# The MLP's relu outputs stored from ScalarE's queue, and the MLP's raw weights loaded and released in halves of a quarter

## Chip, core and metric

The kernel runs on one core of a Trainium2 chip. The metric is the device time of one launch in microseconds (us); the time before is the median of three runs. Engines are named as the profile does: PE is TensorE, DVE is VectorE, ACT is ScalarE, POOL is GpSimd, SP is SyncE. SP computes nothing here; it issues DMAs. ACT and POOL compute and can issue DMAs as well.

## What is computed

One transformer block on 512 tokens of width 2048, in float32: a mixing part (attention with compressed, selected and windowed keys, beside a retention part), then an MLP of hidden width 8192. The change touches the MLP alone:

```python
mix = jnp.concatenate([o_a.astype(x.dtype), o_r], axis=-1) @ w_out[l]
x = x + rms_norm(mix, norm_mix_post[l])
h = rms_norm(x, norm_mlp_pre[l])
u = jnp.square(jax.nn.relu(h @ w_up[l]))          # (512, 2048) @ (2048, 8192)
x = x + rms_norm(u @ w_down[l], norm_mlp_post[l])  # (512, 8192) @ (8192, 2048)
```

## The kernel before

**Precision.** Every float32 operand of a matmul is split into a high part (a cast on ACT to the reduced float32 type, tile `whi`) and a low part (the difference, a subtract on DVE, tile `wlo`). A product is three matmuls: high by high, low by high, high by low (`mm3`).

**Seven products for eight.** Both MLP matmuls are done block by block with the scheme of seven products on 2 by 2 blocks. A block of weights has four raw quarters, named 11, 12, 21 and 22, of 1 MB each ([128, 2048] float32). The products are numbered 0 to 6 and done in the order 0, 1, 2, 5, 4, 3, 6 (`ORDER`). Their weight operands are quarter 11, then 21, then 11 with 12 added, then 22, then 11 with 22 added, then 12 with 22 added, then 11 with 21 added (`ADD` names the quarter added to and the one that is added, `SPLIT` the one that is split). The adds run on DVE in place (L951). In most blocks the add of product 3 is instead a DMA from POOL that accumulates quarter 22 from HBM onto quarter 12 (`late_sum`, L917).

**Phases and slabs.** A product is a phase, and a phase is two slabs (s = 0 and 1), each half of the contraction, of [128, 1024] raw weights and 24 matmuls. `Feed` walks the phases. For a slab `advance` emits the add on DVE (if any), the cast on ACT (L956), and then the subtract on DVE of the slab before (`low`, L931). `slab` keeps it three slabs ahead of the matmuls at most; `whi` and `wlo` have three buffers each. The order of the instructions on each engine is the order in which this code emits them; nothing reorders them.

**Slots.** Raw quarters live in four slots of 1 MB: `low0`, `low1` and two rows of the tile `Y` (three more, `pre0` to `pre2`, are used once at the start). A quarter's slot is given back in `low`, after the subtract of slab 1 of the last phase that uses the quarter. `load` then issues the next quarter from SP (L925), in the order of the phases, up to three phases ahead (`ahead`).

**Up and down.** The up part has 16 blocks of 512 hidden columns, in the order 0, 4, 1, 5, 2, 6, 3, 7, 8, ..., 15. Products 0 and 1 of blocks 0 to 3 and product 0 of block 4 are done early, while the normalisation of the mixing part is still being finished on ACT and DVE (`work3`); their slabs have their own loads. So blocks 0 to 3, when their turn comes, have five phases left: 5, 2, 4, 3, 6. From product 5, which needs 22, such a block goes on to product 2, which needs both 11 and 12. The down part has 16 pieces of seven phases.

**Stores.** Each up block leaves seven hidden tensors, [128, 512] each. One is squared relu of product 1's sum, one of product 4's, one of product 3's (`hidden`: relu and square on ACT, L1122 and L1123, one slab later, the store two slabs after that). Four are sums of them (`sums`, four DVE adds, L1181 to L1184, stored one slab later). `keep_u` (L1126) stores each to `ud` in HBM from SP, 112 stores of 256 KB in all. The down part loads them back (`u_operand`).

**DMA semaphores.** DMAs of the SP and ACT queues share eight completion semaphores (DMAHW0 to DMAHW7), handed round in the order in which the code emits the DMAs. A DMA that takes a semaphore waits until the DMA eight before it, of either queue, has landed, unless its engine already knows that. POOL's DMAs have eight of their own (DMASW).

Of the kernel before, what the change touches and what calls it, by code (L numbers as in the profile page):

```python
# [10 lines left out]
F32 = mybir.dt.float32  # L11
F32R = mybir.dt.float32r
AF = mybir.ActivationFunctionType
ALU = mybir.AluOpType
AX = mybir.AxisListType.X

P = 128
# [95 lines left out]
def block_kernel(ctx: ExitStack, tc: tile.TileContext, x, norm_mix_pre, w_in, cmp_pe_k, cmp_w1_k, cmp_b1_k,  # L113
                 cmp_w2_k, cmp_pe_v, cmp_w1_v, cmp_b1_v, cmp_w2_v, t5_bias, w_out, norm_mix_post, norm_mlp_pre,
                 w_up, w_down, norm_mlp_post, c_rot, c_dec, c_hot, c_misc, out):
    nc = tc.nc
# [22 lines left out]
    ud = dram.tile([7, DFF // 512, P, 512], F32, name="ud")  # L139
# [242 lines left out]
    for q in (2, 3):  # L382
        c = slice(q * 512, (q + 1) * 512)
# [19 lines left out]
    for n in range(4 * NT):  # L403
        t, q = n // 4, n % 4
# [398 lines left out]
    Y = fp.tile([P, NT, DM], F32, name="Y")  # L803
# [60 lines left out]
    ADD = (None, None, (11, 12), (12, 22), (11, 22), None, (11, 21))  # L864
    SPLIT = (11, 21, 11, 12, 11, 22, 11)
    SL = 1024
# [11 lines left out]
    class Ring:  # L878
# [3 lines left out]
        def take(self):  # L882
            self.views.append(self.views.pop(0))
            return self.views[-1]

    class Feed:


# [1 line left out]


        def __init__(self, phases, slots, ahead, short):
            self.phases, self.free, self.ahead, self.lent = phases, list(slots), ahead, []
            self.short = short
            self.n, self.at, self.R, self.ready = 0, 0, {}, {}
            self.loads, self.last = [], {}
            for i, (g, prod, source) in enumerate(phases):
                for q in (SPLIT[prod],) if self.by_dma(i) else (ADD[prod] or ()) + (SPLIT[prod],):
                    if (g, q) not in self.last:
                        self.loads.append((g, q, source, i))  # L900
                    self.last[g, q] = i
            self.held = None

# [5 lines left out]
        def late_sum(self, i):  # L909

            g, prod, source = self.phases[i]
            to, by = ADD[prod]
            src = source(by)
            k = src.shape[1]
            r = self.R[g, to].rearrange("p (k n) -> p k n", k=k)
            for h in (slice(0, k // 2), slice(k // 2, k)):
                nc.gpsimd.dma_start(r[:, h], src[:, h], accum_op=ALU.add)  # L917

        def load(self, most=99):
            while most and self.loads and self.free and self.loads[0][3] <= self.n // 2 + self.ahead:  # L920
                most -= 1
                g, q, source, _ = self.loads.pop(0)
                r = self.R[g, q] = self.free.pop(0)
                src = source(q)
                nc.sync.dma_start(r.rearrange("p (k n) -> p k n", k=src.shape[1]), src)  # L925

        def low(self):
            if self.held is None:
                return
            hi, lo, src, i, s = self.held  # L930
            nc.vector.tensor_sub(lo, src, hi.bitcast(F32))  # L931
            self.ready[2 * i + s] = (hi, lo)
            self.held = None
            if s:
                for q in (11, 12, 21, 22):
                    if self.last.get((self.phases[i][0], q)) == i:
                        r = self.R.pop((self.phases[i][0], q))
                        if all(r is not o for o in self.lent):
                            self.free.append(r)

        def advance(self):
            self.load()
            if self.n == 2 * len(self.phases):
                self.low()
                return
            i, s = divmod(self.n, 2)
            g, prod, _ = self.phases[i]
            c = slice(s * SL, (s + 1) * SL)
            if ADD[prod] and not self.by_dma(i):
                to, by = (self.R[g, q][:, c] for q in ADD[prod])  # L950
                nc.vector.tensor_add(to, to, by)  # L951
            src = self.R[g, SPLIT[prod]][:, c]
            o = 40 if isinstance(g, int) and prod == 6 and s else 0
            hi = hp.tile([P, SL + 128], F32R, name="whi")[:, o:o + SL]
            lo = hp.tile([P, SL + 128], F32R, name="wlo")[:, o:o + SL]
            nc.scalar.copy(hi, src)  # L956
            self.low()
            self.held = hi, lo, src, i, s
            self.n += 1
            if prod == 2 and s and (j := [j for j in range(i, min(i + 5, len(self.phases))) if self.by_dma(j)]):  # L960
                self.late_sum(j[0])
# [137 lines left out]
    NPRO = 4  # L1099
# [3 lines left out]
    phases = [((b, p), p, up_source(b)) for b, p in early]  # L1103
# [19 lines left out]
        nc.scalar.activation(v, v, AF.Square)  # L1123

    def keep_u(k, b, v):
        nc.sync.dma_start(ud[k, b], v)  # L1126

    def up_done(b, p, ps):

# [86 lines left out]
        feed.low()  # L1216
        yield

    feed.load(1)
    for q in range(4):  # L1220
        x_fetch(0, q)
    feed.load(1)
    outs = [x1_out(t) for t in range(NT)]
    beside(ends[0][1](), 2, primed())
    beside(ends[1][1](), 1, x1_chain(0))
# [8 lines left out]
    sxv = [sxp.tile([P, 8, 2 * P], F32R, name=f"sx{i}") for i in range(2)]  # L1234
    prctx = ExitStack()
    prp = prctx.enter_context(tc.tile_pool(name="prim", bufs=1, reuse_waits="tile"))
    feed.lent = [prp.tile([P, 2048], F32, name=f"pre{i}") for i in range(3)]
    feed.free = feed.lent + feed.free
    XA = [tuple(H[:, 0:8, 0:256] for H in (Hh, Hl)), tuple(H[:, 8:16, 0:256] for H in (Hh, Hl)),
          tuple(H[:, 0:8, 256:512] for H in (Hh, Hl)), (sxv[0], sxv[1]), None, None,  # L1240
# [20 lines left out]
    def work3():  # L1261
        yield from pieces("addadaadaa", a=outs[2], d=x1_chain(3))
        yield from both(x1_sums(0), outs[3])
        feed.free += [Y[:, 0, :], Y[:, 2, :]]
        yield from x1_sums(1)

    feed.ahead = len(early)
# [220 lines left out]
```

## Time and profile before

| | us |
|---|---|
| median of 3 runs | 2223.9 (2223.78 to 2226.18) |
| the profiled execution | 2220.96 |
| its span, first to last instruction | 2219.2 |
| PE busy | 2161.8 (97%) |
| DVE busy | 1575.4 (71%) |
| ACT busy | 994.2 (45%) |
| granted TensorE clock, mean | 0.994 |

The span is the time on the core between the first and the last instruction that the profiler recorded; 1.76 us of the execution lie around it. Idle time of PE is 57.4 us in the whole span. The mixing part ends at about 937 us, the up part runs to about 1574 us, the down part's matmuls to about 2200 us, and what follows is the end of the output on DVE. A row of an idle engine names what ended the wait last; a row of DVE or ACT that waits for a DMA names the tile that the DMA fills.

### The profile page before, as it was taken

To read this page: it belongs to the slowest core of one execution; us is meant where nothing else is said; L and a number is where in the kernel's file an instruction comes from. 1 tells how busy PE (TensorE), PEld (TensorE's weight loads), DVE (VectorE), ACT (ScalarE), POOL (GpSimd) and SP (SyncE) were. 2 spreads that over 40 slices of the span, in tenths; PEclk is the share of its full clock that TensorE was granted. 3 is DMA by queue.
4 is the path that set the end of the run, shared out by engine and by line. 5 is a ranking of instruction groups with operands and counts; after the bars stand their busy time and mean duration, and the time that the engine had idled before them with its cause. 6 is when DMAs were issued, how large, how long until landed. Compare 5 with 4: busy or idle time off the path is not lost.

```text
span 2219.2 us, 31801 instructions
## 1 busy us (share of the span) xinstructions
PE 2161.8 (97%) x12787; PEld 1915.4 (86%) x12787; DVE 1575.4 (71%) x1880; ACT 994.2 (45%) x1440; POOL 111.1 (5%) x131
## 2 busy tenths in 40 slices
PE   8999999999999999989999999999999999999995
PEld 7888878878778899989999999999888888888874
DVE  6213555554556533598888878878879999999998
ACT  5213343343332323575555555555664454445443
POOL 0000000000000000000000000000000000000001
PEclk9999999999999999999999999999999999999998
DMA  6543324323224334565655766767675656566664
GB/s 192 136 122 88 93 65 95 95 72 91 81 72 138 98 103 142 186 221 171 207 172 169 225 179 183 190 174 209 223 229 161 216 163 218 160 197 175 192 187 86
DMA packets 248054, 342.67 MB, mean 154 GB/s; under 512 B 14011, under 2 KB 159755, under 8 KB 247009
## 3 DMA queue, kind: packets, MB, share of 16 engines
q1 hardware_dynamic: 213440, 292.43, 40.6%
q0 software_dynamic: 24368, 36.67, 10.3%
q10 hardware_dynamic: 10098, 11.55, 1.5%
q8 instruction: 100, 1.64, 0.3%
q14 instruction: 48, 0.39, 0.1%
HBM read 298.85 MB, written 41.75 MB: 153 GB/s over the span
## 4 chain that ended last, share of the span: by engine, by line
PE 87%; DVE 8%; ACT 2%; issue 1%; DMA 1%; POOL 0%; SPq 0%; DVEq 0%; POOLq 0%; ACTq 0%
PE prod L156 16%; PE prod L155 16%; PE prod L154 16%; PE mm L154 11%; PE mm L156 11%; PE mm L155 11%; DVE wlo L931 2%; PE S L583 2%; PE S L706 1%; PE PT L646 1%; PE oT L741 1%; PE oT L501 1%; PE oT L154 1%; DVE Y L951 1%; DMA low<-in_w_up 1%
## 5 line engine op out<-in xcount | busy, mean ns | idle before, releaser
L956 ACT CAST whi<-low 128x1024 fp32r<-128x1024 f32 x230 | 242.1, 1053 | 277.5 <-PE prod L156 134.9
L155 PE MATMUL prod<-wlo,Hh 128*128 128x512 f32 x896 | 350.5, 391 | 11.5 <-DVE wlo L931 11.4
L956 ACT CAST whi<-Y 128x1024 fp32r<-128x1024 f32 x212 | 222.6, 1050 | 285.7 <-PE prod L156 119.9
L144 DVE TENSOR_TENSOR wlo<-raw,whi 128x1024 fp32r<-128x1024 f32 (+4 forms) x152 | 168.6, 1113 | 255.4 <-ACT whi L143 250.6
L156 PE MATMUL prod<-whi,Hl 128*128 128x512 f32 x896 | 349.4, 390 | 0.0
L154 PE MATMUL prod<-whi,Hh 128*128 128x512 f32 x896 | 349.3, 390 | 0.0
L931 DVE TENSOR_TENSOR wlo<-low,whi 128x1024 fp32r<-128x1024 f32 x230 | 280.1, 1221 | 48.2 <-ACT whi L956 47.3
L156 PE MATMUL prod<-Hh,wlo 128*128 128x256 f32 x1024 | 285.3, 279 | 13.4 <-DVE wlo L931 13.4
L931 DVE TENSOR_TENSOR wlo<-Y,whi 128x1024 fp32r<-128x1024 f32 x212 | 258.4, 1221 | 38.7 <-ACT whi L956 37.7
L154 PE MATMUL prod<-Hh,whi 128*128 128x256 f32 x1024 | 284.7, 278 | 0.3 <-ACT Hh L143 0.3
L155 PE MATMUL prod<-Hl,whi 128*128 128x256 f32 x1024 | 284.0, 277 | 0.9 <-DVE Hl L144 0.9
L143 ACT CAST whi<-raw 128x1024 fp32r<-128x1024 f32 (+4 forms) x152 | 145.6, 960 | 302.2 <-PE mm L155 148.0
L154 PE MATMUL mm<-whi,Hh 128*128 128x416 f32 (+4 forms) x704 | 263.1, 374 | 0.5 <-ACT Hh L143 0.5
L156 PE MATMUL mm<-whi,Hl 128*128 128x416 f32 (+4 forms) x704 | 248.6, 353 | 0.5 <-DVE Hl L144 0.5
L155 PE MATMUL mm<-wlo,Hh 128*128 128x416 f32 (+4 forms) x704 | 248.1, 352 | 0.0
L156 PE MATMUL prod<-sx,wlo 128*128 128x256 f32 x768 | 212.3, 276 | 2.6 <-DVE wlo L931 2.6
L154 PE MATMUL mm<-Hh,whi 128*128 128x512 f32 x512 | 214.7, 419 | 0.1
L154 PE MATMUL prod<-sx,whi 128*128 128x256 f32 x768 | 212.0, 276 | 0.0
L155 PE MATMUL prod<-sx,whi 128*128 128x256 f32 x768 | 212.0, 276 | 0.0
L155 PEld LDWEIGHTS prod<-wlo,Hh 128*128 128x128 f32 x896 | 168.7, 188 | 49.7 <-DVE wlo L931 14.8
L156 PEld LDWEIGHTS prod<-Hh,wlo 128*128 128x128 f32 x1024 | 192.9, 188 | 15.3 <-DVE wlo L931 15.2
L156 PE MATMUL mm<-Hh,wlo 128*128 128x512 f32 x512 | 200.5, 392 | 0.0
(265 smaller groups left out, 3969.9 us busy)
## 6 DMA issues: line engine op xcount, KB each, us to landing
raw<-in_w_in SPq DMA_DIRECT2D x160, 256.0 KB, 3.1
low<-in_w_up SPq DMA_DIRECT2D x38, 1024.0 KB, 6.0
Y<-in_w_up SPq DMA_DIRECT2D x32, 1024.0 KB, 6.3
Y<-in_w_down SPq DMA_DIRECT2D x32, 1024.0 KB, 5.2
low<-in_w_down SPq DMA_DIRECT2D x32, 1024.0 KB, 5.2
Y<-ud SPq DMA_DIRECT2D x49, 512.0 KB, 9.0
ud<-Y SPq DMA_DIRECT2D x77, 256.0 KB, 4.3
raw<-in_w_out SPq DMA_DIRECT2D x32, 416.0 KB, 3.5
```

What stands on the lines that cost most here:

```text
L143: nc.scalar.copy(hi, src)
L144: nc.vector.tensor_sub(lo, src, hi.bitcast(F32))
L154: nc.tensor.matmul(ps, ah, bh, start=first, stop=False)
L155: nc.tensor.matmul(ps, ah, bl, start=False, stop=False)
L156: nc.tensor.matmul(ps, al, bh, start=False, stop=last)
L501: nc.tensor.matmul(hid[:65, :DK], kv[:, l:l + STRIDE * 64 + 1:STRIDE], w1s[l // 16][:, l % 16, :], start=l == 0, stop=l == CBLK - 1)
L583: nc.tensor.matmul(sps[:, :c + L], QT[g][:, h, qs], k, start=True, stop=True)
L646: nc.tensor.transpose(pt[:, e * P:(e + 1) * P], Pt[:, e, rows_of(j)], ident)
L706: nc.tensor.matmul(sps[:, :n], QK[:, 2 + d, rows_of(j)], QK[:, d, j * P:], start=d == 0, stop=d == 1)
L741: nc.tensor.matmul(o[:, :DR], AT[:, a0:a0 + P], vr[:, j, :], start=j == 0, stop=j == i)
L931: nc.vector.tensor_sub(lo, src, hi.bitcast(F32))
L956: nc.scalar.copy(hi, src)
```

## The change

Three things change. `keep_u` issues its store from ACT's queue in place of SP's. A raw quarter becomes two halves of [128, 1024], one for each slab: `Feed.load` issues a DMA of 512 KB for each half, `Feed.low` gives each half's slot back after that slab's subtract, and a phase that needs two new quarters asks for both first halves before the second ones. `feed.ahead` is set to a negative number while the first slabs are primed, so that halves that come free there start no load before the `pre` slots are at hand.

```diff
+    def halved(r):
+        return [r[:, :SL], r[:, SL:]]
...
-            self.phases, self.free, self.ahead, self.lent = phases, list(slots), ahead, []
+            self.phases, self.free, self.ahead, self.lent = phases, [h for r in slots for h in halved(r)], ahead, []
...
-                for q in (SPLIT[prod],) if self.by_dma(i) else (ADD[prod] or ()) + (SPLIT[prod],):
-                    if (g, q) not in self.last:
-                        self.loads.append((g, q, source, i))
+                qs = (SPLIT[prod],) if self.by_dma(i) else (ADD[prod] or ()) + (SPLIT[prod],)
+                fresh = [q for n, q in enumerate(qs) if (g, q) not in self.last and q not in qs[:n]]
+                self.loads += [(g, q, h, source, i) for h in range(2) for q in fresh]
+                for q in qs:
                     self.last[g, q] = i
...
-            while most and self.loads and self.free and self.loads[0][3] <= self.n // 2 + self.ahead:
+            while most and self.loads and self.free and self.loads[0][-1] <= self.n // 2 + self.ahead:
                 most -= 1
-                g, q, source, _ = self.loads.pop(0)
-                r = self.R[g, q] = self.free.pop(0)
+                g, q, h, source, _ = self.loads.pop(0)
+                r = self.R[g, q, h] = self.free.pop(0)
                 src = source(q)
-                nc.sync.dma_start(r.rearrange("p (k n) -> p k n", k=src.shape[1]), src)
+                k = src.shape[1] // 2
+                nc.sync.dma_start(r.rearrange("p (k n) -> p k n", k=k), src[:, h * k:(h + 1) * k])
...
-            if s:
-                for q in (11, 12, 21, 22):
-                    if self.last.get((self.phases[i][0], q)) == i:
-                        r = self.R.pop((self.phases[i][0], q))
-                        if all(r is not o for o in self.lent):
-                            self.free.append(r)
+            for q in (11, 12, 21, 22):
+                if self.last.get((self.phases[i][0], q)) == i:
+                    r = self.R.pop((self.phases[i][0], q, s))
+                    if all(r is not o for o in self.lent):
+                        self.free.append(r)
...
     def keep_u(k, b, v):
-        nc.sync.dma_start(ud[k, b], v)
+        nc.scalar.dma_start(ud[k, b], v)
...
+    feed.ahead = -NPRO
...
-    feed.lent = [prp.tile([P, 2048], F32, name=f"pre{i}") for i in range(3)]
+    feed.lent = [prp.tile([P, SL], F32, name=f"pre{i}") for i in range(6)]
...
-        feed.free += [Y[:, 0, :], Y[:, 2, :]]
+        feed.free += halved(Y[:, 0, :]) + halved(Y[:, 2, :])
```

On PE, DVE and POOL the instructions and their order stay the same; only which slot a quarter lies in differs. The two places where the order moves are these.

SP's queue where the up part goes from block 4 to block 1, before: the four loads (L925) are block 1's quarters 22, 11, 12 and 21, each of 1 MB, and the L1126 rows are stores of block 4.

```order
L1126 DMA ud_77<-Y_5587 128x512 [waits DMAHW7_49,DVE_49,Activation_49]
L925 DMA low1_7097<-in_w_up 128x8x256 [waits DMAHW0_49,DVE_49,Activation_49]
L925 DMA Y_5587<-in_w_up 128x8x256 [waits DMASW7_49,DMAHW1_49,DMASW0_49,DVE_49]
L925 DMA low0_7099<-in_w_up 128x8x256 [waits DMAHW2_49,DVE_49]
L1126 DMA ud_77<-Y_5587 128x512 [waits DMAHW3_49,Activation_49]
L925 DMA Y_5587<-in_w_up 128x8x256 [waits DMAHW4_49]
L1126 DMA ud_77<-Y_5587 128x512 [waits DMAHW5_49,Activation_49]
```

The same place now: block 1's halves are 22 and 22, then the first halves of 11 and 12, then their second halves, then 21 and 21.

```order
L930 DMA Y_5587<-in_w_up 128x4x256 [waits DMAHW0_49,DVE_49,Activation_49]
L930 DMA low1_7097<-in_w_up 128x4x256 [waits DMAHW1_49,DMAHW2_49,DVE_49,Activation_49]
L930 DMA low0_7099<-in_w_up 128x4x256 [waits DMAHW3_49,DMASW7_49,DVE_49]
L930 DMA low1_7097<-in_w_up 128x4x256 [waits DMAHW4_49,DMASW0_49,DVE_49]
L930 DMA Y_5587<-in_w_up 128x4x256 [waits DMAHW5_49,DVE_49]
L930 DMA Y_5587<-in_w_up 128x4x256 [waits DMAHW6_49]
L930 DMA low0_7099<-in_w_up 128x4x256 [waits DMAHW7_49,DVE_49]
L930 DMA Y_5587<-in_w_up 128x4x256 [waits DMAHW0_49]
```

The stores are gone from SP's queue, there are eight loads for four, and the first half of quarter 12 stands ahead of the second half of 11: the wait for DVE that stood before the whole of 12 (the subtract of product 6's slab 1) now stands before the halves of 21, and the four halves of 11 and 12 follow subtracts that come earlier.

ACT's queue where block 1's product 5 ends, before: casts, the relu of block 4's last sum, and the copy of product 5 out of PSUM (L1156).

```order
L1122 ACTIVATE Y_5587<-Y_5587 128x512 [waits DVE_49]
L1123 ACTIVATE Y_5587<-Y_5587 128x512 [waits Activation_49]
L956 CAST whi_8861<-Y_5587 128x1024 [waits DVE_49,PE_49]
L956 CAST whi_8896<-Y_5587 128x1024 [waits DVE_49,PE_49]
L1156 COPY Y_5587<-prod_8826 128x512 [waits DMAHW6_49,PE_49]
L956 CAST whi_8930<-Y_5587 128x1024 [waits DVE_49,PE_49]
```

The same place now:

```order
L1125 ACTIVATE Y_5587<-Y_5587 128x512 [waits DVE_49]
L1126 ACTIVATE Y_5587<-Y_5587 128x512 [waits Activation_49]
L959 CAST whi_8885<-Y_5587 128x1024 [waits DMAHW5_49,DVE_49,PE_49]
L1129 DMA ud_77<-Y_5587 128x512
L959 CAST whi_8920<-low0_7099 128x1024 [waits DVE_49,PE_49]
L1159 COPY Y_5587<-prod_8849 128x512 [waits DMAHW7_49,PE_49]
L1129 DMA ud_77<-Y_5587 128x512
L1129 DMA ud_77<-Y_5587 128x512 [waits DMAHW4_49]
L1129 DMA ud_77<-Y_5587 128x512
L1129 DMA ud_77<-Y_5587 128x512 [waits DMAHW6_49]
L959 CAST whi_8954<-Y_5587 128x1024 [waits DVE_49,PE_49]
```

Five of block 4's seven stores have come in here, four of them in a row ahead of a cast, and two of the four wait for the landing of a DMA that is a weight load of SP. Over the whole program 35 of the 112 stores on ACT wait so for a load of SP, each emitted four to six casts earlier, and four, all of block 0, wait for a sum of DVE.

## Rows read from the trace of the kernel before

**Rows 1.** Busy time in five stretches (normalisation beside the first up phases; up part with blocks 0 to 7 interleaved; rest of the up part; down part; end). Columns: stretch, its length, busy time and instructions of each engine, granted TensorE clock, DMA share, GB/s.

```profile
937.00:1000.00 63.00, 56.10 (x465) 54.87 (x465) 55.81 (x63) 43.21 (x59) 2.68 (x3) 0.97 0.69 228
1000.00:1215.00 215.00, 204.69 (x1779) 203.01 (x1778) 179.13 (x182) 112.63 (x139) 7.68 (x6) 1.00 0.61 183
1215.00:1574.00 359.00, 359.00 (x3163) 359.00 (x3163) 294.68 (x296) 201.84 (x248) 22.92 (x18) 1.00 0.68 190
1574.00:2130.00 556.00, 555.55 (x2457) 460.05 (x2457) 505.46 (x441) 279.90 (x279) 35.48 (x30) 1.00 0.64 193
2130.00:2219.00 89.00, 59.69 (x245) 46.59 (x243) 79.91 (x83) 34.20 (x55) 11.62 (x14) 0.88 0.49 130
```

**Rows 2.** The two longest groups of PE's waits: who waited for whom, total us, times, longest.

```profile
PE prod L156 <- DVE wlo L931: 16.1, 12, 3.8
PE prod L155 <- DVE wlo L931: 11.4, 7, 6.0
```

**Rows 3.** PE's timeline, the matmuls of the up part before which PE stood over 0.5 us: start, duration, instruction, and in brackets the idle time and what ended it.

```profile
983.86 0.39 PE L156 MATMUL prod<-Hh,wlo 128*128 128x256 f32 x1 [1.19 <-DVE wlo L931]
996.35 0.58 PE L156 MATMUL prod<-Hh,wlo 128*128 128x256 f32 x1 [3.78 <-DVE wlo L931]
1031.96 0.38 PE L156 MATMUL prod<-Hh,wlo 128*128 128x256 f32 x1 [1.11 <-DVE wlo L931]
1038.62 0.38 PE L156 MATMUL prod<-Hh,wlo 128*128 128x256 f32 x1 [0.79 <-DVE wlo L931]
1066.93 0.39 PE L156 MATMUL prod<-sx,wlo 128*128 128x256 f32 x1 [0.75 <-DVE wlo L931]
1074.73 0.38 PE L156 MATMUL prod<-Hh,wlo 128*128 128x256 f32 x1 [1.92 <-DVE wlo L931]
1136.01 0.38 PE L156 MATMUL prod<-sx,wlo 128*128 128x256 f32 x1 [0.99 <-DVE wlo L931]
1143.80 0.38 PE L156 MATMUL prod<-Hh,wlo 128*128 128x256 f32 x1 [1.94 <-DVE wlo L931]
1204.97 0.39 PE L156 MATMUL prod<-sx,wlo 128*128 128x256 f32 x1 [0.88 <-DVE wlo L931]
1212.77 0.38 PE L156 MATMUL prod<-Hh,wlo 128*128 128x256 f32 x1 [1.94 <-DVE wlo L931]
```

**Rows 4.** DVE's timeline around the adds of product 2 that waited for a load (the four rows that name a DMA), with the subtracts around the second of them.

```profile
1029.54 1.23 DVE L951 TENSOR_TENSOR low<-low,Y 128x1024 f32<-128x1024 f32 x1 [2.92 <-DMA Y<-in_w_up]
...
1055.51 2.50 DVE L931 TENSOR_TENSOR wlo<-low,whi 128x1024 fp32r<-128x1024 f32 x2
...
1060.74 1.22 DVE L931 TENSOR_TENSOR wlo<-low,whi 128x1024 fp32r<-128x1024 f32 x1
1064.52 1.23 DVE L951 TENSOR_TENSOR Y<-Y,low 128x1024 f32<-128x1024 f32 x1 [2.55 <-DMA low<-in_w_up]
...
1067.40 1.22 DVE L951 TENSOR_TENSOR Y<-Y,low 128x1024 f32<-128x1024 f32 x1
...
1073.46 1.22 DVE L931 TENSOR_TENSOR wlo<-Y,whi 128x1024 fp32r<-128x1024 f32 x1
...
1133.59 1.23 DVE L951 TENSOR_TENSOR Y<-Y,low 128x1024 f32<-128x1024 f32 x1 [2.79 <-DMA low<-in_w_up]
...
1202.56 1.22 DVE L951 TENSOR_TENSOR Y<-Y,low 128x1024 f32<-128x1024 f32 x1 [2.69 <-DMA low<-in_w_up]
```

**Rows 5.** SP's timeline, the issues of block 1's quarters 11 and 12.

```profile
1051.82 0.38 SPq L925 DMA_DIRECT2D Y<-in_w_up  x1
1058.05 0.37 SPq L925 DMA_DIRECT2D low<-in_w_up  x1
```

**Rows 6.** The DMA issues of the short stretch 1058.0 to 1058.4: size and us from issue to landing.

```profile
low<-in_w_up SPq DMA_DIRECT2D x1, 1024.0 KB, 6.4
```

**Rows 7.** The page's DMA issues: 1 MB loads of w_up, 512 KB loads of the mixing part, and the relu stores; count, size, median us from issue to landing.

```profile
low<-in_w_up SPq DMA_DIRECT2D x38, 1024.0 KB, 6.0
...
ud<-Y SPq DMA_DIRECT2D x77, 256.0 KB, 4.3
...
raw<-in_w_in SPq DMA_DIRECT2D x24, 512.0 KB, 4.6
```

**Rows 8.** ACT's timeline: a store issued from ACT's queue at the end of the mixing part (ACTq is ACT's sequencer), and the copy and the cast of block 1 between which the four stores now stand.

```profile
949.30 0.63 ACT L1008 ACTIVATE jk<-Y 128x512 f32<-128x512 f32 x1
949.31 0.34 ACTq L1012 DMA_DIRECT2D out<-Y  x1
...
1074.58 0.58 ACT L1156 COPY Y<-prod 128x512 f32<-128x512 f32 x1
1076.02 1.05 ACT L956 CAST whi<-Y 128x1024 fp32r<-128x1024 f32 x1 [0.86 <-DVE Y L951]
```

**Rows 9.** The stores of the relu outputs on SP's sequencer: durations in ns, least, median and most, and first and last start.

```profile
L1126 SPq DMA_DIRECT2D ud<-Y x77: 319/338/2945, 1023.8 to 1581.9; - x77
```

**Rows 10.** ACT's and DVE's timelines beside the normalisation: a cast that waited for a load, and what followed on both engines.

```profile
977.81 1.05 ACT L956 CAST whi<-low 128x1024 fp32r<-128x1024 f32 x1 [2.36 <-DMA low<-in_w_up]
979.17 0.64 ACT L1122 ACTIVATE xh<-xh 128x512 f32<-128x512 f32 x1 [0.32 <-DVE xh L1143]
...
978.46 0.68 DVE L1143 TENSOR_TENSOR xh<-prod,xh 128x512 f32<-128x512 f32 x1
...
981.45 1.23 DVE L144 TENSOR_TENSOR Hl<-Y,Hh 128x1024 fp32r<-128x1024 f32 x1 [1.71 <-ACT Hh L143]
```

More of the change, by code (lines that the diff above doesn't have):

```diff
@@ L913, in late_sum @@
             src = source(by)
[L914 to L917, printed above, removed]
+            k = src.shape[1] // 2
+            for h in range(2):
+                nc.gpsimd.dma_start(self.R[g, to, h].rearrange("p (k n) -> p k n", k=k), src[:, h * k:(h + 1) * k],
+                                    accum_op=ALU.add)
         def load(self, most=99):
-            while most and self.loads and self.free and self.loads[0][3] <= self.n // 2 + self.ahead:
+            while most and self.loads and self.free and self.loads[0][-1] <= self.n // 2 + self.ahead:
                 most -= 1
-                g, q, source, _ = self.loads.pop(0)
-                r = self.R[g, q] = self.free.pop(0)
+                g, q, h, source, _ = self.loads.pop(0)
+                r = self.R[g, q, h] = self.free.pop(0)
                 src = source(q)
-                nc.sync.dma_start(r.rearrange("p (k n) -> p k n", k=src.shape[1]), src)
+                k = src.shape[1] // 2
+                nc.sync.dma_start(r.rearrange("p (k n) -> p k n", k=k), src[:, h * k:(h + 1) * k])
         def low(self):
@@ L947, in advance @@
             g, prod, _ = self.phases[i]
-            c = slice(s * SL, (s + 1) * SL)
             if ADD[prod] and not self.by_dma(i):
-                to, by = (self.R[g, q][:, c] for q in ADD[prod])
+                to, by = (self.R[g, q, s] for q in ADD[prod])
                 nc.vector.tensor_add(to, to, by)
-            src = self.R[g, SPLIT[prod]][:, c]
+            src = self.R[g, SPLIT[prod], s]
             o = 40 if isinstance(g, int) and prod == 6 and s else 0
@@ L1217, in primed @@
         yield
-    feed.load(1)
+    feed.load(2)
     for q in range(4):
         x_fetch(0, q)
-    feed.load(1)
+    feed.load(2)
+    feed.ahead = -NPRO
     outs = [x1_out(t) for t in range(NT)]
```

## The prediction

> **What bounds the kernel now.** I read the stretches first, since the change lives in the MLP alone. From 1215 to 1574 us PE is busy for all of 359.00 us, and in the down part for 555.55 of 556 [rows 1]. There is nothing to win in either. A faster load only makes a slot full earlier. PE loses 10.3 us in the stretch 1000 to 1215, 6.9 beside the normalisation, and 29 at the end [rows 1]. The groups of waits then say whom PE waits for in the MLP: the subtract `wlo` on DVE and hardly anything else [rows 2]. A wait on DVE is not yet a reason, so I looked at each such wait in time [rows 3] and at what DVE had been doing before it [rows 4].
>
> In the stretch 1000 to 1215 PE's waits come at four places, each of two waits: 1.11 + 0.79 = 1.90 us, 0.75 + 1.92 = 2.67, 0.99 + 1.94 = 2.93 and 0.88 + 1.94 = 2.82 [rows 3], in all 10.32, the whole loss of that stretch. A little before each of them DVE itself stands, for 2.92, 2.55, 2.79 and 2.69 us, and what ends it is the landing of a load [rows 4]. It is the first add of product 2, and it waits for quarter 12. At the second place SP issues quarter 11 at 1051.82 and quarter 12 only at 1058.05 [rows 5]; 12 lands 6.4 us later [rows 6], at 1064.45, and the add starts at 1064.52 [rows 4]. The second issue follows directly on a subtract: the pair that starts at 1055.51 ends at 1058.01 [rows 4]. That is product 6's slab 1 of the block before, whose end gives the slot back. So the load is late because its slot is late, not because SP was held by a store.
>
> **The halves: when do the loads come now?** Product 3's second subtract gave a slot at 1051.8 and product 6's first one ends about half way through the pair, at 1055.51 + 1.25 = 1056.8 [rows 4, 5]. In the new order the first halves of 11 and 12 take what product 3 gives back, and the second halves take what product 6's slab 0 gives back. For a half's landing I have two rows: 4.6 us for 512 KB loads elsewhere and 6.0 for a whole quarter [rows 7]. I take 6.0, the worse, and 0.4 more for the second of two issues [rows 5]. First half of 12: 1051.8 + 0.4 + 6.0 = 1058.2. DVE could use it when its subtract before is done, at 1060.74 + 1.22 = 1061.96 [rows 4]: 3.8 us to spare. Second halves: 1056.8 + 0.4 + 6.0 = 1063.2. Their add is at 1067.40 now [rows 4] and would come 2.55 earlier, at 1064.85: 1.6 us to spare, 3.0 with 4.6. Blocks 2 and 3 repeat this place with the same steps, and at block 4 (the first place) 11 and 12 move to earlier subtracts in the same way.
>
> So DVE's stall goes, at each place for all of its length. What is late next? DVE works without a pause from 1064.52 until PE's second wait has ended at 1074.7 [rows 3, 4]: all of that moves up by the length of the stall, and PE's waits end that much earlier. The gain is the smaller of the two sums at each place: 1.90 (of 2.92), 2.55 (of 2.67), 2.79 (of 2.93), 2.69 (of 2.82). **Sum: 9.93 us.** The 0.12 to 0.14 left at three places are DVE's own work. PE has no idle time afterwards up to the end of the down part [rows 1], so what is won there stays won, as long as its loads keep up, and they come earlier than before everywhere.
>
> **What the halves add.** 137 more issues on SP at 0.38 us [rows 5], 52 us, less 112 stores at 0.34 [rows 9], 38 us. SP computes nothing and now holds loads alone; its share of the sum is nothing. The bytes are the same. A DMA may now wait for one eight DMAs before it that holds half as many bytes. On SP 87 of the 274 loads wait for a store on ACT in this way, but nearly all for one emitted five or more casts earlier. Such a cast comes once a slab. A slab of 24 matmuls is 24 x 359.00 / 3163 = 2.72 us [rows 1], so five are 13.6 us, against 4.3 for a store to land [rows 7]. I put it at nothing.
>
> The Trainium skill speaks against this part: "DMA: Bandwidth & Descriptors", under "Rules for kernel authors", wants at least 1 MiB in a DMA for full bandwidth, and its section on the anatomy of a DMA gives a fit (for DMAs issued from GpSimd) of 2.0 us and the bytes over 436 GB/s. By that fit, an estimate from the page, two halves end to end take 6.4 us where a quarter takes 4.4. The rows have the same direction, 9.2 against 6.0 [rows 7].
>
> **The stores on ACT.** No store moves in the program's order, but each now stands in ACT's queue with a cast behind it. A store issued from ACT took 0.34 us, beside an activation that ran at the same time [rows 8]. So one store costs between 0 (hidden under ACT's work or its waits) and 0.34 us, all 112 between 0 and 38 us. I take 0, since ACT is busy for 201.84 of 359.00 us in the up part [rows 1]. Bursts are another matter: four in a row are 1.4 us. Where they meet the four places, the copy ahead of them starts at 1074.58 and the cast behind at 1076.02 [rows 8], so they may push that cast by up to 0.6 us; its subtract comes two DVE operations later, so nothing waits for it. In general a cast may start when PE leaves a buffer, and is needed two slabs later, 5.4 us; cast and subtract take 1.05 + 1.22 [rows 4, 8]. That leaves 3.2 us for a burst of 1.4. I keep 0 to 2 us for this in the range. Stores on SP blocked no late load, so moving them wins nothing by itself; it keeps them out of the way of loads that now want to go earlier.
>
> **Beside the normalisation** the trace has a bait: ACT stands 2.36 us for a load [rows 10], and PE waits 1.19 and 3.78 us a little later [rows 3]. But the next thing that ACT does at 979.17 waits for DVE's add of 978.46, and that chain ends DVE's 1.71 us of idling [rows 10]. An earlier load fills ACT's idle time and ends there. I count nothing. At the end PE's waits are behind 79.91 us of DVE work in 89 [rows 1]; they stay.
>
> **The number.** The profiled execution took 2220.96, its span 2219.2. Span after: 2219.2 - 9.93 = 2209.3; with the 1.76 around it 2211.0. The median of the runs stands 2.9 above the profiled one, so on its scale 2223.9 - 9.9 = **2214.0**.
>
> **Rivals.**
> - **More is won** (0.10). The load at 977.81 was in the chain after all. DVE's idle 1.71 us there goes as well [rows 10]: 2212.3. With all of the two waits (4.97) 2209.0. Against it: ACT's next step waits for DVE.
> - **Only the first wait of each place goes** (0.05): DVE catches up less than I think, because it then waits for PE's sums. 1.11 + 0.75 + 0.99 + 0.88 = 3.73 [rows 3]: 2220.2. Against it: DVE's work there shows no pause.
> - **Two halves are slower than one quarter** (0.05). If two land as two 512 KB loads end to end, 9.2 us [rows 7], the second halves are there at 1056.8 + 9.2 = 1066.0, 1.2 after they are wanted. Four times 1.2 is 4.8: 9.9 - 4.8 = 5.1, 2218.8; with the store traffic between them, none of the gain. The page above has this rule. Against it: other loads overlap, two quarters issued together do not take twice 6.0 in this kernel.
> - **The loads don't come earlier** (0.03): the shared semaphores tie SP to ACT's stores, or a slot is not really free. 2223.9.
> - **ACT is held in a store** (0.05), the one that ends slower. 35 stores wait for the landing of a load of SP. If that load is late, ACT stands, and the casts behind it. It decides from 3.2 us, the room found above. A hold of the 6.0 us of a landing on top of a burst of 1.4 is 4.2 over it; once in each of the 16 blocks 67 us, 2223.9 - 9.9 + 67 = 2281; in one of four blocks 2231. Against it: the load was emitted four to six casts before, 11 us or more.
> - **My forecast**: 0.72, by itself from 2212 to 2217.
>
> The Trainium skill has a rule for the other half of the change too: under "Issuing engines are not separate DMA queues" the same page says that issuing from several engines saves only the sequencer's time. My sum takes nothing from it, and no row here shows otherwise.
>
> **Range and chances.** 8 in 10: the forecast's own 2212 to 2217, down to 2209.0 for more, up to 2219.3 for a part of the gain lost. Runs of this kernel lie 2.4 us apart, so 0.2% (4.4 us) is about what a measurement can tell from no change. Faster than 2219.5: forecast, more, and half of the halves' rival, about 0.83. Within 4.4 us: 0.12. Slower: 0.05.
>
> **What would show it.** Right: no add L954 (now) of product 2 that waits for a DMA, and PE's waits at the four places down to some 0.1 to 0.3 us each; those at 984, 996 and at the end as before; PE still full from there on. The stores land in about 4 us, 0.34 each on ACT. Wrong: casts on ACT that start right behind a store while PE waits for them; adds that still wait for a half; new waits of PE in the down part, where the loads are half as long; or less DVE idling with the same PE waits, which would mean that DVE's work, not the load, was the bound.

## The result, and the profile after

The changed kernel takes 2210.82 us in the median of 4 runs (2210.67 to 2212.10), the kernel before 2223.84 (2220.63 to 2226.18, 4 runs). The ratio is 0.9944, 95% interval 0.9926 to 0.9961: 13.0 us less, where 9.9 were forecast. Nine executions, with those of the last experiment, lie between 2209.51 and 2212.10. One execution of the kernel before, of 2462.63 us at a mean granted clock of 0.847, is left out everywhere. The two profiled executions differ by less than the medians: 2220.96 and 2212.10, spans 2219.2 and 2210.3, so 8.9 us. What is read from traces first has to explain these 8.9; the other 4 are a question of their own, taken up further down.

The busy time by stretches, cut at the same work as [rows 1]:

```profile
937.00:1000.00 63.00, 56.17 (x464) 54.80 (x465) 55.63 (x63) 43.27 (x60) 1.65 (x3) 0.97 0.71 234
1000.00:1215.00 215.00, 213.64 (x1861) 213.05 (x1860) 188.38 (x192) 116.58 (x143) 7.68 (x6) 1.00 0.62 187
1215.00:1564.00 349.00, 349.00 (x3075) 349.00 (x3075) 284.73 (x286) 197.43 (x242) 22.92 (x18) 1.00 0.68 191
1564.00:2121.00 557.00, 556.56 (x2464) 461.03 (x2464) 506.35 (x441) 280.44 (x280) 35.48 (x30) 1.00 0.66 194
2121.00:2210.00 89.00, 58.91 (x244) 45.99 (x242) 79.58 (x82) 34.19 (x55) 11.61 (x14) 0.87 0.49 124
```

PE's idle time in 1000 to 1215 fell from 10.3 us to 1.36; in each other stretch it is within 0.8 us of what it was. PE's timeline, its waits of 0.4 us and more in that stretch, and the last two ahead of it:

```profile
983.98 0.39 PE L156 MATMUL prod<-Hh,wlo 128*128 128x256 f32 x1 [1.18 <-DVE wlo L936]
996.47 0.58 PE L156 MATMUL prod<-Hh,wlo 128*128 128x256 f32 x1 [3.80 <-DVE wlo L936]
1070.50 0.39 PE L156 MATMUL prod<-Hh,wlo 128*128 128x256 f32 x1 [0.45 <-DVE wlo L936]
1136.69 0.38 PE L156 MATMUL prod<-Hh,wlo 128*128 128x256 f32 x1 [0.46 <-DVE wlo L936]
1203.48 0.39 PE L156 MATMUL prod<-Hh,wlo 128*128 128x256 f32 x1 [0.45 <-DVE wlo L936]
```

Of the eight waits of the four places [rows 3] three are left, of 0.45, 0.46 and 0.45 us, each the second of its place; the first place has none. That is 10.32 - 1.36 = 8.96 us won. The waits beside the normalisation (1.18 and 3.80) are unchanged. The matmul that ends the fourth place started at 1212.77 [rows 3] and now starts at 1203.48, 9.29 earlier.

DVE's timeline at the second place (block 1), to be held against [rows 4]:

```profile
1053.93 1.22 DVE L936 TENSOR_TENSOR wlo<-Y,whi 128x1024 fp32r<-128x1024 f32 x1
1055.21 1.23 DVE L936 TENSOR_TENSOR wlo<-low,whi 128x1024 fp32r<-128x1024 f32 x1
...
1060.30 1.22 DVE L954 TENSOR_TENSOR low<-low,low 128x1024 f32<-128x1024 f32 x1
...
1063.17 1.22 DVE L954 TENSOR_TENSOR Y<-Y 128x1024 f32<-128x1024 f32 x1
...
1069.23 1.22 DVE L936 TENSOR_TENSOR wlo<-Y,whi 128x1024 fp32r<-128x1024 f32 x1
```

No add of product 2 (1060.30, 1063.17) has a bracket that names a DMA, or any bracket. No instruction of DVE from 1000 us to the end of the down part waits for a DMA now. The two subtracts of product 6 are now two rows, at 1053.93 and 1055.21: between them stands the point that the halves use. SP's timeline there:

```profile
1047.57 3.05 SPq L930 DMA_DIRECT2D low<-in_w_up  x2
1055.18 0.92 SPq L930 DMA_DIRECT2D Y<-in_w_up  x2
```

The first row is the two first halves of 11 and 12, the second row their second halves, issued at the end of the subtract of slab 0 (1053.93 + 1.22 = 1055.15) and not after that of slab 1, which ends at 1056.44. The halves of quarter 21 follow that one. How long the second halves take, from the list of DMA issues of 1055 to 1056:

```profile
Y<-in_w_up SPq DMA_DIRECT2D x2, 512.0 KB, 4.6
```

And the stores on ACT, the operation's durations in ns (least, median, most) with first and last start, and the page's line for them:

```profile
L1129 ACTq DMA_DIRECT2D ud<-Y x77: 326/327/1606, 1026.0 to 1575.4; - x77
```

```profile
ud<-Y ACTq DMA_DIRECT2D x77, 256.0 KB, 3.2
```

They take ACT's queue 0.33 us each (one of them 1.6) and land in 3.2 us, 4.3 before [rows 7]. From 940 us on PE's waits name DVE, and none of them ACT.

### The profile page after: what moved, and what is told of

It is laid out like the page before. It is cut to its first block, busy times and chain, and to the rows that moved or that the text cites. A ratio compares the mean times of both kernels' runs of the same rounds, so it can differ in the third digit from the quotient of the medians.

```text
span 2210.3 us, 31917 instructions
## 1 busy us (share of the span) xinstructions
PE 2161.1 (98%) x12787; PEld 1915.7 (87%) x12787; DVE 1574.9 (71%) x1880; ACT 994.3 (45%) x1440; POOL 110.0 (5%) x131
## 3 DMA queue, kind: packets, MB, share of 16 engines
q0 software_dynamic: 24368, 36.67, 10.3%
q8 instruction: 100, 1.64, 0.3%
## 4 chain that ended last, share of the span: by engine, by line
PE 88%; DVE 8%; issue 2%; ACT 1%; DMA 1%; POOL 0%; SPq 0%; DVEq 0%; ACTq 0%; POOLq 0%
PE prod L156 16%; PE prod L155 16%; PE prod L154 16%; PE mm L154 11%; PE mm L156 11%; PE mm L155 11%; DVE wlo L936 2%; PE S L583 2%; DVE low L954 1%; PE S L706 1%; PE PT L646 1%; PE oT L741 1%; PE oT L501 1%; PE oT L154 1%; DVE acc L1369 1%
```

## The experiments

Two halves of the change come first: which of them is worth the time, the stores or the halves? Then what it is about the halves: the earlier giving back, the order, or the size. Then the 4 us between medians and traces. Last, a version that goes on from the change. The theory of the prediction is called the slot theory: a half starts when its own slab's subtract is done, so it is there when DVE wants it.

**The halves alone.** The changed kernel with one line of the kernel before:

```diff
     def keep_u(k, b, v):
-        nc.scalar.dma_start(ud[k, b], v)
+        nc.sync.dma_start(ud[k, b], v)
```

> The halves alone; the relu outputs are stored from SyncE's queue again. Slot theory (the gain comes from loads that start earlier because slots come back by halves): same as the changed kernel, 2211 us within 1, and the four places keep PE waits of 0 to 0.5 us each. Store theory (SyncE was held by stores, and moving them is what lets loads start earlier): back near 2224, with adds of product 2 that wait for quarter 12. If the stores cost ScalarE time, this kernel is faster than the changed one, by at most 2 us.

Measured: 2212.13 us (2210.84 to 2212.21), ratio 0.9942 (0.9930 to 0.9955). The four places show PE waits of 0, 0.46, 0.46 and 0.45. The halves alone give the gain, within the spread of the runs; the store theory (SP was held by its stores) falls.

**The stores alone.** The kernel before with the other form of that line.

> The stores on ScalarE alone; raw quarters are loaded and given back whole, as before. Slot theory: same as before, 2224 us, 0 to 2 slower, with the four waits of DVE for quarter 12 (2.5 to 2.9 us each) still there. Store theory: 2211, and those waits gone.

Measured: 2224.04 us (2222.17 to 2228.07), ratio 0.9998 (0.9989 to 1.0006). DVE's timeline, the adds of product 2:

```profile
1032.58 1.23 DVE L951 TENSOR_TENSOR low<-low,Y 128x1024 f32<-128x1024 f32 x1 [4.82 <-DMA Y<-in_w_up]
...
1068.39 1.23 DVE L951 TENSOR_TENSOR Y<-Y,low 128x1024 f32<-128x1024 f32 x1 [2.98 <-DMA low<-in_w_up]
...
1137.19 1.23 DVE L951 TENSOR_TENSOR Y<-Y,low 128x1024 f32<-128x1024 f32 x1 [2.54 <-DMA low<-in_w_up]
...
1207.85 1.23 DVE L951 TENSOR_TENSOR Y<-Y,low 128x1024 f32<-128x1024 f32 x1 [2.77 <-DMA low<-in_w_up]
```

All four waits for quarter 12 are there, one of them longer in this execution. Moving the stores is worth nothing that can be measured, and costs nothing either.

**The cut alone.** The changed kernel, loads in the order 11, 11, 12, 12, both halves given back after slab 1:

```diff
-                self.loads += [(g, q, h, source, i) for h in range(2) for q in fresh]
+                self.loads += [(g, q, h, source, i) for q in fresh for h in range(2)]
...
-                if self.last.get((self.phases[i][0], q)) == i:
-                    r = self.R.pop((self.phases[i][0], q, s))
-                    if all(r is not o for o in self.lent):
-                        self.free.append(r)
+                if s and self.last.get((self.phases[i][0], q)) == i:
+                    for h in range(2):
+                        r = self.R.pop((self.phases[i][0], q, h))
+                        if all(r is not o for o in self.lent):
+                            self.free.append(r)
```

> The changed kernel, but each quarter's two halves are loaded one right after the other (11, 11, 12, 12) and both are given back only after slab 1, as before the change: loads are cut in two, and nothing else of the halves is left. Slot theory: quarter 12's first half is issued when the quarter was before, and only lands earlier, since it is half as long: 4.2 to 5.0 us after its issue in place of 6.4. DVE's wait of 2.6 us before the first add of product 2 shrinks to 0.6 to 1.2 and the gain is about 60 per cent: 2215 to 2218 us. Size theory (that a load is shorter is all there is): 2211, as the changed kernel. If only the earlier giving back counts: 2224.

Measured: 2210.98 us (2209.92 to 2212.58), ratio 0.9940 (0.9926 to 0.9953), the whole gain. By its number that is the size theory. The trace says that the expectation had misread this kernel. SP's timeline, quarters 11 and then 12 of block 1:

```profile
1047.68 3.04 SPq L930 DMA_DIRECT2D Y<-in_w_up  x2
1055.30 1.66 SPq L930 DMA_DIRECT2D low<-in_w_up  x2
```

and DVE's, the two subtracts of product 6 and the first add of product 2:

```profile
1054.05 2.50 DVE L936 TENSOR_TENSOR wlo<-low,whi 128x1024 fp32r<-128x1024 f32 x2
...
1060.41 1.22 DVE L955 TENSOR_TENSOR Y<-Y,low 128x1024 f32<-128x1024 f32 x1
```

The first half of 12 leaves at 1055.30, when the first of the two subtracts is over and the second (to 1056.55) has just begun. The second half leaves only behind the second subtract: the row of two ends at 1056.96, and an issue takes 0.37 [rows 5]. The code gives it back later, but SP's wait is on the last reader of the bytes that the DMA writes, and those bytes had been read. What the code gives back when only sets the order in SP's queue; the cut itself makes the wait finer. So this run doesn't tell size from start, and another had to.

**The order alone.** The changed kernel with only the second piece of that diff.

> The changed kernel, but both halves of a quarter are given back only after slab 1; the new order of the loads (both first halves, then both second halves) stays. Slot theory: first halves of 11 and 12 go into what product 3's second subtract gives back, second halves into what product 6's second subtract gives back; the latter land about 1 us before their add is due: 2211 to 2213 us. If the giving back by halves is what counts: 2218 to 2224, with the second add of product 2 waiting for a load.

Measured: 2211.22 us (2210.30 to 2211.47), ratio 0.9940 (0.9927 to 0.9952), PE's waits 0, 0.46, 0.46 and 0.45. With the run before: neither the order nor the place in the code where a half is given back matters to the time. They do move one half: the second half of 12 follows the second subtract of the pair in both runs, 0.9 us later than in the changed kernel (2.5 us after the start of the pair, against 1.7), and is still in time.

**Cut across the slabs.** The kernel before with the stores on ACT and two DMAs for a quarter, each of which takes every other row block of both slabs:

```diff
-                nc.sync.dma_start(r.rearrange("p (k n) -> p k n", k=src.shape[1]), src)
+                to = r.rearrange("p (k n) -> p k n", k=src.shape[1])
+                for h in range(2):
+                    nc.sync.dma_start(to[:, h::2], src[:, h::2])
```

> The kernel before with the stores on ScalarE, each raw quarter loaded by two DMAs of 512 KB as in the changed kernel, but cut across the slabs: one takes every other row block of both slabs, the other the rest. So the loads are as small and as many as in the changed kernel, but each half needs the subtracts of both slabs to be done before it may start, and each slab's add needs both halves. Slot theory (a half may start when its own slab's subtract is done): no gain, 2224 us within 2, and DVE still waits 2 to 3 us for quarter 12 at four places. Size theory (two smaller DMAs are there sooner than one large one): 2211 to 2216.

Measured: 2221.28 us (2215.88 to 2222.53), ratio 0.9984 (0.9975 to 0.9993), between the two theories and nearer to the first. SP's issues of quarter 12 and DVE's adds of product 2:

```profile
1058.29 0.92 SPq L927 DMA_DIRECT2D low<-in_w_up  x2
```

```profile
1029.28 1.22 DVE L953 TENSOR_TENSOR low<-low,Y 128x1024 f32<-128x1024 f32 x1 [1.63 <-DMA Y<-in_w_up]
...
1063.63 1.23 DVE L953 TENSOR_TENSOR Y<-Y,low 128x1024 f32<-128x1024 f32 x1 [1.42 <-DMA low<-in_w_up]
...
1131.62 1.23 DVE L953 TENSOR_TENSOR Y<-Y,low 128x1024 f32<-128x1024 f32 x1 [1.71 <-DMA low<-in_w_up]
...
1201.11 1.22 DVE L953 TENSOR_TENSOR Y<-Y,low 128x1024 f32<-128x1024 f32 x1 [1.63 <-DMA low<-in_w_up]
```

Cut so, a half needs both subtracts before it may start, and an add needs both halves. Now the load waits for both subtracts again and leaves at 1058.29, as it did before the change (1058.05, [rows 5]). Its add starts 5.3 us after that, where a whole quarter took 6.5 (1064.52 - 1058.05, [rows 4, 5]). So two DMAs of half the size are 1.1 us sooner than one. DVE's four waits sum to 6.39 us, against 10.95 before [rows 4] and 0 in the changed kernel. PE's waits at the four places are 0.79, 1.64, 1.82 and 1.92, in all 6.17, against 10.32 and 1.36: of the 8.96 us that the traces show, size gives 4.15 and the finer wait, put on top of it, 4.81. The finer wait is of two parts here, the load's for one subtract and the add's for one half; no run separates them. Of the time itself size gives 2.5 us and the finer wait 10.5, and that is more than the waits account for. The granted clock goes with it: the three executions of this version with a mean of 0.994 took 2215.88 to 2218.50 us, the eight with 0.992 or 0.993 took 2219.84 to 2222.53. The next experiment looks into that.

**Where the other 4 us are.** They are two gaps: the profiled execution of the kernel before is 2.9 us under its median, that of the changed kernel 1.3 over its own. Each execution has a mean granted clock beside its time. In the 38 executions of the kernel before that were run beside the experiments, the median is 2222.7 us at 0.994 (5 of them), 2223.8 at 0.993 (16), 2225.4 at 0.992 (16) and 2227.6 at 0.991 (1). The profiled execution of the prediction, with 2220.96, was among the shortest. So the kernel before was profiled three times more.

> The kernel before once more, for a second profile. Clock theory (the medians differ by more than the two profiled executions do, since in most executions of the kernel before TensorE falls to its lower clock for some us after one or two of the eight waits): about 2224 us, with a stretch at the lower clock behind at least one wait of the four places. Chance theory (the profiled execution was fast for another reason, spread over the kernel): no such stretch there.

> The kernel before, a third profile. In the runs so far an execution of it takes longer the lower its mean granted clock (about 2222.6 at 0.994, 2223.9 at 0.993, 2225.4 at 0.992, 2227.6 at 0.991). Clock theory: at 2222 us or more there is a stretch at the lower clock behind a wait of the four places that the two faster profiled executions (2219.7 and 2221.0) lack; at 2221 or less there is none. Other theory: the extra time lies elsewhere.

> The kernel before, a fourth profile; the clock theory and the other one expect of it what they expect of the third: a stretch at the lower clock between 1010 and 1215 us if the time is 2222 us or more, none if it is 2221 or less.

Measured: 2219.66, 2225.64 and 2224.87 us. The first was itself a short one and could only show that a short one lacks the stretch, which it does. The other two decide it. Stretches behind the second and third place, of the kernel before in the profile of the prediction, and then in the second and the third of the three new ones (the granted clock is the third number from the right):

```profile
1076.30:1079.20 2.90, 2.90 (x28) 2.90 (x27) 2.90 (x3) 1.61 (x2) 0.00 (x0) 1.00 0.04 8
1145.80:1148.80 3.00, 3.00 (x28) 3.00 (x28) 3.00 (x4) 1.71 (x3) 0.00 (x0) 1.00 0.00 0
```

```profile
1076.30:1079.20 2.90, 2.90 (x15) 2.90 (x15) 2.90 (x3) 1.08 (x2) 0.00 (x0) 0.50 0.00 0
1147.80:1150.80 3.00, 3.00 (x16) 3.00 (x16) 3.00 (x4) 1.64 (x3) 0.00 (x0) 0.50 0.00 0
```

```profile
1076.10:1078.80 2.70, 2.70 (x14) 2.70 (x14) 2.70 (x3) 1.04 (x1) 0.00 (x0) 0.50 0.00 0
1147.60:1150.50 2.90, 2.90 (x16) 2.90 (x15) 2.90 (x3) 1.27 (x2) 0.00 (x0) 0.50 0.00 0
```

In both longer executions PE runs at 0.50, the lower of its two levels (1.2 GHz), for some 3 us about 1 us after the second wait of a place, and does half the matmuls in the time: 15 in 2.90 us for 28. Four such stretches, some 3 us each: about 1.5 us lost in each, 3 in an execution, out of spans that are 4.7 and 3.9 longer (2223.9 and 2223.1 against 2219.2). Two more differences lie ahead of the four places, and nearly cancel. The longer executions are 1.1 and 1.6 us ahead early on (DVE's instruction at 102.24 us starts at 101.10 and 100.65), and they lose about as much behind the wait of 3.72 us beside the normalisation, where the clock of 993 to 1003 is 0.66 in place of 0.83. That loss isn't tied to the change: three of the eight profiles of kernels cut along the slabs have 0.66 there too. The waits ahead of the four stretches are no longer than in the short execution. PE's timeline of the second of the three new profiles:

```profile
1074.95 0.38 PE L156 MATMUL prod<-Hh,wlo 128*128 128x256 f32 x1 [1.83 <-DVE wlo L931]
...
1146.06 0.39 PE L156 MATMUL prod<-Hh,wlo 128*128 128x256 f32 x1 [1.93 <-DVE wlo L931]
```

1.83 and 1.93, against 1.92 and 1.94 in the execution without [rows 3]. What decides whether the clock falls behind such a wait isn't settled. The run with the stores alone had two such stretches, the one cut across the slabs one. So of six profiles without the cut along the slabs four have a clock of 0.98 or 0.99 over 1010 to 1215 us. Of the eight with it all have 1.00.

The gap of the changed kernel is smaller and needs no cause of its own: its profiled execution is the longest of the nine. Its second profile (2209.51 us) is 1.7 us ahead at the instruction named above, 100.67 against 102.40.

**The changed kernel and a step beyond it.** In the stretch 2121 to 2210 of the changed kernel DVE is busy for 79.58 of 89 us, and PE loses 11 us behind it. With halves there is time to let a DMA do an add of product 6: it may start when product 4's subtract of that slab is done, and the cast wants it three slabs later. In the last two blocks:

```diff
+    LATE = [("down", 7, 0), ("down", 7, 1)]
...
+        def late_half(self, i, s):
+            g, prod, source = self.phases[i]
+            to, by = ADD[prod]
+            src = source(by)
+            k = src.shape[1] // 2
+            nc.gpsimd.dma_start(self.R[g, to, s].rearrange("p (k n) -> p k n", k=k), src[:, s * k:(s + 1) * k],
+                                accum_op=ALU.add)
...
             self.held = None
+            if self.phases[i][1] == 4 and self.phases[i][0] in LATE:
+                self.late_half(next(j for j in range(i, i + 4) if self.phases[j][:2] == (self.phases[i][0], 6)), s)
```

> The changed kernel, and in the last two blocks of the down part product 6's add is no longer done by DVE: after product 4's subtract of a slab, a DMA from POOL accumulates that half of quarter 21 onto quarter 11, which the halves make possible in time. It takes four adds of 1.13 us from DVE, which is busy without a pause from 2117 us on. If the end is bound by DVE's chain, 3 to 4.5 us are won of the changed kernel, 2206.5 to 2208; if by the length of the last sums alone, or if the accumulating DMAs (about 6 us each) come too late, 0 to 1 us, or a loss of up to 3.

> As the run before, and product 4's adds of the last two blocks go to POOL's DMAs as well: eight adds, 9.0 us of DVE's work in the last 95 us. DVE's chain: 5 to 8 us won of the changed kernel, 2203 to 2206. If TensorE or the accumulating DMAs set the end from there: no more than the run before.

Measured: 2210.78 us for product 6 alone (2209.09 to 2211.48, ratio 0.9941, 0.9928 to 0.9955), 2213.65 with product 4 as well (2212.56 to 2213.97, ratio 0.9953, 0.9940 to 0.9965). Beside the changed kernel's 2210.7 the first wins nothing that can be told, and the second loses 2.9 us; 3 to 4.5 and 5 to 8 less were expected if DVE's chain sets the end. PE's timeline and ACT's of the second:

```profile
2126.51 0.80 PE L154 MATMUL prod<-whi,Hh 128*128 128x512 f32 x1 [2.89 <-ACT whi L972]
...
2170.16 0.50 PE L154 MATMUL prod<-whi,Hh 128*128 128x512 f32 x1 [2.10 <-ACT whi L972]
```

```profile
2125.42 1.04 ACT L972 CAST whi<-low 128x1024 fp32r<-128x1024 f32 x1 [7.48 <-DMA low<-in_w_down]
```

The issues of 2110 to 2128 us in the same run:

```profile
low<-in_w_down POOLq DMA_DIRECT2D x3, 512.0 KB, 11.2
```

The accumulating DMAs, now more of them on one queue, take 11.2 us where the expectation counted 6: the cast waits 7.48 us for one, and PE behind it. The clock falls behind that wait too: 0.89 over 2120 to 2150 us, where the changed kernel has 1.00. By these two figures, an estimate, PE loses up to another 3.3 us. The first version was run once more beside the changed kernel.

> The changed kernel once more, beside the run after it: 2210.8 within 1, no stretch at the lower clock between 1010 and 1215 us.

> The changed kernel with product 6's adds of the last two blocks moved to POOL's DMAs, once more and beside the changed kernel on one chip. Its profile lost 2.3 us less of TensorE's time in the wait before the last product, and its first five executions had the median of the changed kernel. If the gain is real: 1 to 3 us under the run before. If it is given back by a wait elsewhere: within 0.7 of it.

Measured: the changed kernel 2210.62 us (2209.51 to 2211.62, ratio 0.9940, 0.9927 to 0.9952), with no stretch at the lower clock between 1010 and 1215 us; the version 2209.34 (2208.90 to 2210.42, ratio 0.9935, 0.9921 to 0.9949). Over all executions the medians are 2210.7 (9) and 2209.8 (10), 0.9 us apart, and their ranges overlap. PE's longest group of waits, in the changed kernel and then in the version:

```profile
PE prod L155 <- DVE wlo L936: 11.4, 7, 6.0
```

```profile
PE prod L155 <- DVE wlo L946: 8.4, 7, 3.7
```

So 3.0 us less of waiting gives about 1 us of time in the medians. DVE's timelines say where some of the rest is. An instruction ahead of the last two blocks starts at 2087.11 in this run of the changed kernel and at 2088.48 in the version, the last one at 2203.23 and 2202.55: the end is 2.05 us shorter, and the 1.37 us lost before lie where both do the same work. The two earlier profiles give 2.05 as well (2089.59 and 2088.64, then 2205.70 and 2202.70). So the step wins about 2 us at the end of the program; the spread of whole executions, 2.6 us in nine of the changed kernel, can hide it.

## Why the prediction held, and where it was off

**What bounds the kernel** was right: the four places lost their waits, and no other stretch changed. PE was full from 1215 to the end of the up part and still is (349.00 of 349.00 us).

**When the loads come** was right to a few tenths. The prediction's times are on the clock of the kernel before; by the second place the changed kernel is 1.6 us ahead (the subtract of slab 0 starts at 1053.93, where the pair started at 1055.51 [rows 4]). Second halves forecast for 1056.8: at 1055.18, that is 1056.8. First add of product 2 forecast for 1061.96: at 1060.30, that is 1061.9. Second add forecast for 1064.85: at 1063.17, that is 1064.8. The landing of 6.0 taken for a half was too long: 4.6, so the room was larger than counted. But the giving back in the code, on which the prediction rested this, isn't the cause: with it undone one of the halves leaves 0.9 us later, still in time, and the time of the kernel is the same. The cut makes the wait finer by itself.

**What is late next** was a little off. 0.12 to 0.14 us were to stay at three places; 0.45 stay, since no row of DVE between 1060.30 and the subtract of 1069.23 that ends the wait has a bracket: it is DVE's own work, as the prediction has it. Why 0.45 and not 0.13 is not shown. The sum of 9.93 is 8.96 in PE's waits of the profiled executions, 0.97 less; by the start of the matmul that ends the fourth place it is 9.29.

**The number** is where the forecast went wrong in size. The measured 2210.82 lies below the forecast's own 2212 to 2217; it is inside the stated range only because a rival that did not come about, more won beside the normalisation, had been given room down to 2209.0. That part is luck. The step that failed is the last one: it put the 2.9 us between the profiled execution and the median on top as a constant that both kernels have. They were not constant: in the longer executions that were profiled some 3 us are stretches at the lower clock behind the very waits that the change takes away. None of the eight profiles with the cut along the slabs has such a stretch, and the medians differ by 13.0, not by 9.9. That the median as a whole is made up so is argued from two longer profiles and from the clocks beside the times, not shown for each execution. The changed kernel's profiled execution stands over its median instead, by 1.3. A hint of it stood in the rows: the one stretch of the up part with a longer wait, 3.78 us [rows 3], is also the only one of that part with a clock under 1.00, 0.97 [rows 1].

**Two halves slower than one quarter** is refuted: two are there in 5.3 us where one takes 6.5. By the fit that the Trainium skill gives in "DMA: Bandwidth & Descriptors", in the section on the anatomy of a DMA and for DMAs issued from GpSimd, two end to end would take an estimated 6.4 where one takes 4.4; the measurement decides here. Halves are not short everywhere: the two of quarter 21, issued right behind these, took 6.2 and 7.9 us to land, with no wait behind them.

**More is won** came near by its size, but not by its place: the waits beside the normalisation are 1.18 and 3.80, as before. **Only the first wait of each place**: refuted, the second ones shrank from between 0.79 and 1.94 us to between 0 and 0.46. **The loads don't come earlier**: refuted by the issue at 1055.18. **ACT held in a store**: no PE wait from 940 us on names ACT, and the kernel with the stores on SP is not faster. The stores' cost of 0 to 2 us on ACT, taken as 0, measured as nothing either way. ACT does wait 2.43 us at 1587.64 now for a stored tensor that is loaded back, 0.38 with the stores on SP; PE is not later for it: its idle time in the down part is 0.44 us, 0.45 before [rows 1].

## What to carry to other kernels

Where an engine waits for a load, ask first which bytes the load's own wait is on: a transfer cut along the boundary that its readers have starts as early as the first part of its slot is read, without any change of the code that hands slots out, and half the size lands sooner besides. Shown here: cut along the slabs 13 us, cut across them 2.5, both with the clock's part in them. And a short wait of TensorE can cost more than its idle row says, in executions other than the one profiled (some 3 us here); compare granted clocks and medians before a profiled time is carried over to the median.

## What the runs showed of the hardware beyond what was expected

TensorE's clock fell from 1.00 to 0.50 for about 3 us behind waits of 1.8 to 1.9 us in two of four profiles of the kernel before, and stayed at 1.00 behind waits of the same length in the other two.

With PE full and the clock at 1.00 a stretch can still run at two speeds. The same slabs of the up part, first in the kernel before and then in the changed kernel:

```profile
1002.00:1024.00 22.00, 22.00 (x196) 22.00 (x196) 18.24 (x17) 10.97 (x14) 0.00 (x0) 1.00 0.30 95
```

```profile
1002.00:1024.00 22.00, 22.00 (x189) 22.00 (x189) 18.28 (x17) 10.30 (x13) 0.00 (x0) 1.00 0.34 109
```

196 and 189 matmuls in 22 us, 112 and 116 ns each, in both without a gap. It is 0.8 us over eight slabs here. It does not come from the change: the second profile of the changed kernel has 196 there too. Nothing in the trace says what sets it.
